# Four PSUM banks in one ring for projections and attention values, in place of three and one

## The chip, the cores and the metric

The kernel runs on one core of a Trainium2 chip. The metric is the device time of one execution in microseconds (us). Five engines work side by side, each through its own queue in order: TensorE (PE in the profile, with its weight loads as PEld), VectorE (DVE), ScalarE (ACT), GpSimd (POOL), and SyncE (SP), which here only starts transfers. Matmul results land in PSUM, which this kernel divides into eight banks of 128 partitions x 512 float32 numbers.

## The reference

One layer of a backbone for 1024 latent tokens and 256 context tokens of width 1024. Every token is normalised and modulated, then one input projection feeds three groups of heads, whose results are gated, put side by side and projected back:

```python
zl = jnp.split(hl @ w_in[l], PROJ_SPLITS, axis=-1)
zc = jnp.split(hc @ w_in[l], PROJ_SPLITS, axis=-1)
kc, vc = heads(zc[5]), heads(zc[6])
ya = short_conv_branch(zl[0], zl[1], zl[2], zl[3], conv_sc[l])
yb = neighbourhood_attention(heads(zl[4]), heads(zl[5]), heads(zl[6]), kc, vc, rpb[l])
yb = yb * jax.nn.silu(zl[7])
yc = conformer_branch(zl[8], zl[9], zl[10], conv_cf[l], conv_cf_b[l], ln_cf_g[l], ln_cf_b[l])
y = jnp.concatenate([ya, yb, yc], axis=-1) @ w_out[l]
x = x + gate[:, None, :] * y
```

`neighbourhood_attention` has 8 heads of 64 columns; each query looks at an 8 x 16 window of the 16 x 64 grid and at all context keys in one softmax.

## The kernel before, in words

Every matmul of a projection or of attention is split into high and low parts to keep float32 precision: a projection tile is 8 steps of three matmuls (lines 329 to 331), summed in one PSUM bank over 24 matmuls.

**Attention** goes by pairs of heads (four pairs), and in a pair by 16 blocks of 128 queries, 8 for each head. For block i `scores` (lines 596, 597) writes the scores to `ps_s`, DVE adds the bias and takes the minimum (601), ACT takes the exponential (604), DVE a reciprocal (605), POOL scales (606). Two blocks later `transposed` (615) turns the weights on PE into `ps_t`, and ACT and DVE (619, 620) copy them out as high and low parts `pw`. One step after that `values` (627) multiplies them with the values into a tile `po`. Two blocks, an even and an odd one, share a `po` tile; after the odd one `fold` reads it in three instructions: ACT 572, then DVE 576 and 578. The next even block opens the next `po`.

`attend` weaves these steps into projections. After each attention step three units of a projection (nine matmuls of 512 columns) follow on PE, so that a projection tile is spread over some three blocks. What remains of a pair's attention after its 16 steps runs as a coroutine during the projections of the next pair. Two more coroutines run beside attention: `conv_part`, the 31 taps of a convolution on DVE (line 692), and, in the last pair, `cf_norm`, which opens eight PSUM tiles of its own for transposes on PE (713 and 734) and waits in between for statistics and scaling on DVE and POOL.

**Order of work.** PE issues in the order in which the program is written. Outside `start` the order on DVE, ACT, POOL and SP is made by a planner at build time, which also hands out buffers: a tile of a pool gets the buffer that, by its plan, was freed first, and the first instruction that writes the new tile waits for the last readers of the old one.

**PSUM before.** `ps_s` and `ps_t` take two banks each. The pool `ps_z` has three banks; all projections, the value projection and `cf_norm` draw from it. The pool `ps_o` has one bank, for `po` alone. In `start`, `zb` holds the three `ps_z` banks and the `ps_o` bank for the first projections and for the matmuls of line 1000, which only keep PE busy. After attention the output projection has four banks `ps_f` in place of `ps_s` and `ps_t`.

Of the kernel before, what the change touches and what calls it, by code (L numbers as in the profile page):

```python
# [8 lines left out]
F32 = mybir.dt.float32  # L9
# [4 lines left out]
PSUM = bass.MemoryType.PSUM  # L14
DRAM = bass.MemoryType.DRAM

P = 128
# [5 lines left out]
HALF = 512  # L23
# [42 lines left out]
class Builder:  # L66
# [464 lines left out]
    def attention(self, pair):  # L531
        blocks = [(h, b) for h in range(2) for b in range(NB)]
        n = len(blocks)
        st = [None] * n
        vt, sg, kt = self.vt, self.sg, self.kt
        y = self.t2.tile([P, T], F32, name="yb", bufs=1)
        for i in range(n + LAG + 1):
            if i < n:
                h, b = blocks[i]
                if i == 0:  # L540
                    qv = [self.q_first]
                if b % 4 == QAH and i + 4 < n:
                    hn, bn = blocks[i + 4 - QAH]
                    qv.append(self.q_parts(hn, bn // 4))
                if b in (2, 4, 5) and 2 * pair + h < 7:
                    self.bias_tables(2 * pair + h + 1, (b - 1) // 2)
                st[i] = self.scores(kt, h, b, qv[i // 4])
            j = i - LAG
            if 0 <= j < n:
                st[j] = self.transposed(*st[j])  # L550
            j -= 1
            if j >= 0:
                h, b = blocks[j]
                if b % 2 == 0:
                    po = self.ps_o.tile([P, 2, 2, P], F32, name="po", tag="po")
                self.values(vt, h, b, st[j], po[:, b % 2])
                if b % 2 == 1:
                    self.fold(h, b // 2, po, y)
                if h == 1 and b % 4 == 3:
                    yg, sgg = (v.rearrange("p (r c) -> p r c", c=GW)[:, :, 8 * b - 24:8 * b + 8] for v in (y, sg))  # L560
                    self.nc.vector.tensor_tensor(out=yg, in0=yg, in1=sgg, op=ALU.mult)
                    if b == NB - 1:
                        self.nc.sync.dma_start(out=self.yd[2 + pair], in_=y)
            yield 2.5
# [487 lines left out]
    def build(self):  # L1052
# [13 lines left out]

        att = ExitStack()
        e, r = inp.enter_context, att.enter_context
        self.ps_z = e(self.pool("ps_z", 3, PSUM, side="right"))
        self.ps_o = e(self.pool("ps_o", 1, PSUM, side="right"))  # L1070
        self.u_cf, self.acc_cf, self.m_sc = {}, {}, {}
        hc = r(self.pool("hctx", 1, side="right"))
        self.h_ctx = [hc.tile([P, KT, TC], F32R, name=f"hc{i}") for i in range(2)]
# [7 lines left out]
        self.sp_b = q(self.pool("sp_b", 1, side="left"))  # L1081
        self.sp_w = stw.enter_context(self.pool("sp_w", 2, side="right"))
        zb = [self.ps_z.tile([P, HALF], F32, name="ps_z", tag="z") for _ in range(3)]
        zb.append(self.ps_o.tile([P, 2, 2, P], F32, name="po", tag="po").rearrange("p a b c -> p (a b c)"))

        def attn_pool():
            stw.close()
# [47 lines left out]
        with ExitStack() as st:  # L1135
            e = st.enter_context
# [78 lines left out]
```

## Time and profile before

| | |
|---|---|
| median of 3 runs | 612.09 us (611.95 to 612.26) |
| profiled execution | 610.97 us, of which 609.2 us are the span of the profile |
| PE busy, idle | 589.7 us, 19.5 us |
| DVE, ACT, POOL busy | 400.7, 245.9, 182.1 us |
| granted TensorE clock | 0.997 |
| attention of the four pairs, on PE | 166 to 222, 252 to 308, 338 to 393, 424 to 479 us |
| last projections, output projection | to 513 us, to the end |

The profile's busy time of PE counts a matmul until its modelled end. Matmuls overlap: one of 512 columns counts 0.39 us, but the next one starts 0.23 us after it. Idle time of PE in the profile is therefore what is left beyond the tail of the instruction before.

### The profile page before, as it was taken

How to read it: one execution, taken by the hardware profiler on the slowest of the kernel's cores; microseconds unless marked ns; L12 is line 12 of the kernel's file. 1: busy time of each engine (PE TensorE's matmuls, PEld its weight loads, DVE VectorE, ACT ScalarE, POOL GpSimd, SP SyncE). 2: the span in 40 equal slices, each digit the busy share in tenths (PEclk: the TensorE clock that was granted, in tenths of full speed). 3: DMA queues.
4: the chain of work that ended last, by engine and by line, in shares of the span. 5: the costliest groups of instructions: out<-in, count | busy, mean ns of one | idle time of the engine just before them, and what ended most of it. 6: DMA issues, size and time to landing. Idle time of an engine off the chain costs nothing.

```text
span 609.2 us, 8937 instructions
## 1 busy us (share of the span) xinstructions
PE 589.7 (97%) x3101; PEld 493.8 (81%) x3101; DVE 400.7 (66%) x681; ACT 245.9 (40%) x470; POOL 182.1 (30%) x194
## 2 busy tenths in 40 slices
PE   7899999999999999999999999999999999999995
PEld 5566888888888888888888888888788888888885
DVE  4466988765676699578897666936889447383222
ACT  2555822111455432544423554425645334124222
POOL 1021233000443222333112332113433370099311
PEclk9999999999999999999999999999999999999998
DMA  8992585976533136332145242172301454951122
GB/s 285 356 335 63 190 272 169 115 156 180 121 86 77 24 91 167 75 81 54 41 138 128 48 113 56 45 215 65 81 19 36 137 166 147 341 177 36 70 103 104
DMA packets 97170, 78.64 MB, mean 129 GB/s; under 512 B 26507, under 2 KB 80869, under 8 KB 96997
## 3 DMA queue, kind: packets, MB, share of 16 engines
q1 hardware_dynamic: 95397, 71.51, 42.4%
q10 hardware_dynamic: 1728, 6.55, 3.0%
q8 instruction: 25, 0.41, 0.3%
q14 instruction: 20, 0.16, 0.1%
HBM read 55.93 MB, written 14.29 MB: 115 GB/s over the span
## 4 chain that ended last, share of the span: by engine, by line
PE 84%; DVE 5%; ACT 3%; issue 2%; DMA 2%; POOL 2%; SPq 1%; POOLq 0%; DVEq 0%; ACTq 0%
PE ps_z L329 14%; PE ps_z L331 14%; PE ps_z L330 14%; PE po L627 5%; PE ps_f L878 5%; PE ps_f L879 5%; PE ps_f L877 5%; PE ps_t L615 4%; PE ps_z L419 3%; PE ps_z L421 3%; PE ps_s L596 3%; PE ps_z L420 3%; PE ps_s L597 2%; DMA wr<-in_w_in 2%; PE ps_h L279 1%
## 5 line engine op out<-in xcount | busy, mean ns | idle before, releaser
L329 PE MATMUL ps_z<-h,wh 128*128 128x512 f32 x384 | 151.1, 394 | 0.0
L331 PE MATMUL ps_z<-h,wl 128*128 128x512 f32 x384 | 150.3, 391 | 0.0
L330 PE MATMUL ps_z<-h,wh 128*128 128x512 f32 x384 | 149.8, 390 | 0.0
L130 POOL TENSOR_TENSOR wl<-wr,wh 128x512 fp32r<-128x512 f32 x44 | 60.8, 1384 | 167.3 <-ACT wh L129 160.3
L606 POOL TENSOR_SCALAR pr<-pr,sm 128x640 f32<-128x640 f32 (+1 forms) x64 | 56.6, 884 | 138.2 <-DVE sm L605 118.1
L331 PEld LDWEIGHTS ps_z<-h,wl 128*128 128x128 f32 x384 | 72.1, 188 | 16.1
L330 PEld LDWEIGHTS ps_z<-h,wh 128*128 128x128 f32 x384 | 72.1, 188 | 12.4
L329 PEld LDWEIGHTS ps_z<-h,wh 128*128 128x128 f32 x384 | 72.1, 188 | 12.1
L692 DVE SCALAR_TENSOR_TENSOR acc<-t,half_w,acc 128x1024 f32<-128x1024 f32 x60 | 81.1, 1351 | 1.2
L619 ACT ACTIVATE pw<-ps_t 128x640 fp32r<-128x640 f32 (+1 forms) x64 | 43.5, 680 | 90.1 <-PE ps_t L615 89.9
L601 DVE CUSTOM_DVE_ANT_0 ps_s<-ps_s,bt 128x640 f32<-128x640 f32 (+1 forms) x64 | 50.9, 796 | 29.4 <-PE ps_s L597 27.1
L620 DVE TENSOR_TENSOR pw<-ps_t,pw 128x640 fp32r<-128x640 f32 (+1 forms) x64 | 50.4, 788 | 16.0 <-ACT pw L619 15.8
L604 ACT ACTIVATE pr<-ps_s,mn 128x640 f32<-128x640 f32 (+1 forms) x64 | 49.0, 766 | 19.4 <-DVE mn L601 18.5
L627 PE MATMUL po<-pw,vt 128*128 128x256 f32 x304 | 51.3, 297 | 4.1 <-DVE yb L578 3.1
L878 PE MATMUL ps_f<-wol,y 128*128 128x512 f32 (+1 forms) x136 | 51.6, 379 | 0.0
L879 PE MATMUL ps_f<-woh,y 128*128 128x512 f32 (+1 forms) x136 | 51.5, 379 | 0.0
L877 PE MATMUL ps_f<-woh,y 128*128 128x512 f32 (+1 forms) x136 | 51.5, 379 | 0.0
L129 ACT ACTIVATE wh<-wr 128x512 fp32r<-128x512 f32 x46 | 29.0, 630 | 42.3 <-PE ps_z L330 21.0
L627 PEld LDWEIGHTS po<-pw,vt 128*128 128x128 f32 x304 | 40.5, 189 | 6.4 <-issue 4.7
L615 PE MATMUL ps_t<-ident,pr 128*128 128x128 f32 x304 | 43.6, 272 | 0.0
L596 PE MATMUL ps_s<-kt,qd 128*128 128x384 f32 (+1 forms) x128 | 39.6, 331 | 0.5 <-ACT pr L604 0.4
L615 PEld LDWEIGHTS ps_t<-ident,pr 128*128 128x128 f32 x304 | 35.6, 141 | 1.4 <-issue 0.4
(177 smaller groups left out, 923.9 us busy)
## 6 DMA issues: line engine op xcount, KB each, us to landing
wr<-in_w_in SPq DMA_DIRECT2D x52, 256.0 KB
wa<-in_w_ada SPq DMA_DIRECT2D x16, 512.0 KB
qd<-qn SPq DMA_DIRECT2D x32, 256.0 KB
vd<-t SPq DMA_DIRECT2D x20, 256.0 KB
x_in<-in_x SPq DMA_DIRECT2D x8, 512.0 KB
t<-in_w_ada SPq DMA_DIRECT2D x16, 256.0 KB
vt<-vd SPq DMA_DIRECT2D x32, 128.0 KB
fraw<-in_w_out SPq DMA_DIRECT2D x8, 512.0 KB
```

What stands on the lines that cost most here:

```text
L130: i2 = (eng or nc.vector).tensor_tensor(out=lo, in0=src, in1=f32(hi), op=ALU.subtract)
L329: nc.tensor.matmul(ps, lhsT=wh, rhs=hh, start=(k == 0), stop=False)
L330: nc.tensor.matmul(ps, lhsT=wh, rhs=hl, start=False, stop=False)
L331: self.last = nc.tensor.matmul(ps, lhsT=wl, rhs=hh, start=False, stop=(k == KT - 1))
L596: nc.tensor.matmul(win, lhsT=q[:, b % 4], rhs=kwin, start=(i == 0), stop=(i == 1))
L606: nc.gpsimd.tensor_scalar(out=pr, in0=pr, scalar1=sm, scalar2=0.5, op0=ALU.mult, op1=ALU.mult)
L615: nc.tensor.transpose(out=pt[:, c * P:(c + 1) * P], in_=pr[:, c * P:(c + 1) * P], identity=self.ident)
L627: self.nc.tensor.matmul(po, lhsT=vt[:, vi, h], rhs=pw[:, c], start=(c == 0), stop=(c == n - 1))
L692: self.after_pe(nc.vector.scalar_tensor_tensor(out=acc, in0=u[:, t:t + T], scalar=self.half_w[:, 2 * t + ct:2 * t + ct + 1], in1=acc, op0= ...
L877: nc.tensor.matmul(ps, lhsT=yh, rhs=wh[:, ch], start=(first and i == 0), stop=False)
L878: nc.tensor.matmul(ps, lhsT=yh, rhs=wl[:, ch], start=False, stop=False)
L879: nc.tensor.matmul(ps, lhsT=yl, rhs=wh[:, ch], start=False, stop=(last and i == len(chs) - 1))
```

## The change

`po` is no longer a pool of its own. `ps_z` has four banks, `po` is drawn from it under the same tag as the projections' tiles and seen as [2, 2, 128] for each partition, and the fourth tile of `zb` comes from it too. The number of banks, every instruction and its operands' shapes stay as they were.

```diff
                 if b % 2 == 0:
-                    po = self.ps_o.tile([P, 2, 2, P], F32, name="po", tag="po")
+                    po = self.ps_z.tile([P, HALF], F32, name="po", tag="z").rearrange("p (a b c) -> p a b c", a=2, b=2)
...
-        self.ps_z = e(self.pool("ps_z", 3, PSUM, side="right"))
-        self.ps_o = e(self.pool("ps_o", 1, PSUM, side="right"))
+        self.ps_z = e(self.pool("ps_z", 4, PSUM, side="right"))
...
         zb = [self.ps_z.tile([P, HALF], F32, name="ps_z", tag="z") for _ in range(3)]
-        zb.append(self.ps_o.tile([P, 2, 2, P], F32, name="po", tag="po").rearrange("p a b c -> p (a b c)"))
+        zb.append(self.ps_z.tile([P, HALF], F32, name="ps_z", tag="z"))
```

## The prediction

> **What bounds the kernel now.** I read the page first, then the waits of PE, then PE's order of time around the waits found.
>
> ```profile
> span 609.2 us, 8937 instructions
> PE 589.7 (97%) x3101; PEld 493.8 (81%) x3101; DVE 400.7 (66%) x681; ACT 245.9 (40%) x470; POOL 182.1 (30%) x194
> ...
> PEclk9999999999999999999999999999999999999998
> ```
>
> PE sets the time: busy for 97% of the span, at the full clock nearly everywhere. Whatever makes PE start its attention work sooner shortens the span, if nothing later gives it back. So the question is where PE waits for a `po` bank. The view of waits by engine, for PE (total us, times, longest):
>
> ```profile
> PE po L627 <- DVE yb L578: 3.1, 4, 1.0
> ...
> PE ps_z L734 <- DVE t L724: 0.9, 2, 0.5
> PE po L627 <- ACT pw L619: 0.8, 1, 0.8
> ...
> PE ps_s L596 <- ACT pr L604: 0.4, 2, 0.2
> ```
>
> Four times the first values matmul waits for line 578, the last reader of the `po` before. These are idle times after the modelled end of the transposes, so they are short of the true delay. I measure that by starts (a count of less than five after x is cut by the window asked for). PE's order of time, first an undelayed block with five transposes and one with four, then the delayed ones:
>
> ```profile
> 177.46 0.71 PE L615 MATMUL ps_t<-ident,pr 128*128 128x128 f32 x5
> 177.92 0.84 PE L627 MATMUL po<-pw,vt 128*128 128x256 f32 x5
> ...
> 447.58 0.60 PE L615 MATMUL ps_t<-ident,pr 128*128 128x128 f32 x4
> 447.93 0.61 PE L627 MATMUL po<-pw,vt 128*128 128x256 f32 x3
> ```
>
> ```profile
> 173.31 0.71 PE L615 MATMUL ps_t<-ident,pr 128*128 128x128 f32 x5
> 174.81 0.83 PE L627 MATMUL po<-pw,vt 128*128 128x256 f32 x5 [0.80 <-ACT pw L619]
> ...
> 302.94 0.60 PE L615 MATMUL ps_t<-ident,pr 128*128 128x128 f32 x4
> 304.56 0.83 PE L627 MATMUL po<-pw,vt 128*128 128x256 f32 x5 [1.03 <-DVE yb L578]
> ...
> 438.80 0.71 PE L615 MATMUL ps_t<-ident,pr 128*128 128x128 f32 x5
> 440.36 0.83 PE L627 MATMUL po<-pw,vt 128*128 128x256 f32 x5 [0.86 <-DVE yb L578]
> ...
> 462.44 0.71 PE L615 MATMUL ps_t<-ident,pr 128*128 128x128 f32 x5
> 463.90 0.48 PE L627 MATMUL po<-pw,vt 128*128 128x256 f32 x2 [0.76 <-DVE yb L578]
> ...
> 470.22 0.71 PE L615 MATMUL ps_t<-ident,pr 128*128 128x128 f32 x5
> 471.06 0.59 PE L627 MATMUL po<-pw,vt 128*128 128x256 f32 x3
> ```
>
> Undelayed, values start 0.46 us after the first of five transposes, 0.35 us after the first of four. At 174.81 the distance is 1.50, so 1.04 us are lost; at 304.56 it is 1.62, 1.27 lost; at 440.36, 463.90 and 471.06 1.10, 1.00 and 0.38. Ten even blocks in all show this, the first and the last of them above; the other five lose 0.25, 0.20, 0.25, 0.66 and 0.37. **The sum is 6.5 us: 3.67 in pairs 0 to 2 and 2.85 in pair 3.** The row at 174.81 names ACT, but DVE tells otherwise:
>
> ```profile
> 171.05 0.82 DVE L620 TENSOR_TENSOR pw<-ps_t,pw 128x640 fp32r<-128x640 f32 x1 [0.45 <-ACT pw L619]
> ...
> 174.25 0.41 DVE L578 TENSOR_TENSOR yb<-po,yb 64x256 f32<-64x256 f32 x1
> ...
> 302.67 1.29 DVE L692 SCALAR_TENSOR_TENSOR acc<-t,half_w,acc 128x1024 f32<-128x1024 f32 x1
> 303.99 0.43 DVE L578 TENSOR_TENSOR yb<-po,yb 64x256 f32<-64x256 f32 x1
> ```
>
> The weights `pw` of that block were ready at 171.87, 2.94 us early; line 578 ended at 174.66, 0.15 us before PE went on. The third row shows why a fold is late: it stands in DVE's queue behind a tap of the convolution that nobody waits for.
>
> **The change, part by part.** It adds and removes no instruction and no transfer; no DMA is moved past another by the edit itself. It removes one wait: an even block's values no longer wait for the fold of the pair of blocks just before. It adds two of the same kind: `po` may wait for a projection's sink, and a projection may wait for a fold.
>
> *The wait removed.* Ten delays, 6.5 us. What is late next when a delay goes? PE then reaches the next scores earlier by as much, and these wait for `ps_s`, which ACT must have read (line 604). The largest delay of pairs 0 to 2 that has scores behind it, and the tightest place of all:
>
> ```profile
> 174.71 0.79 ACT L604 ACTIVATE pr<-ps_s,mn 128x640 f32<-128x640 f32 x1
> ...
> 176.87 0.33 PE L596 MATMUL ps_s<-kt,qd 128*128 128x384 f32 x1
> ```
>
> ```profile
> 464.82 0.80 ACT L604 ACTIVATE pr<-ps_s,mn 128x640 f32<-128x640 f32 x1 [0.87 <-DVE mn L601]
> ...
> 466.62 0.33 PE L596 MATMUL ps_s<-kt,qd 128*128 128x384 f32 x1
> ```
>
> After the first delay `ps_s` is free at 175.50 and scores start at 176.87: 1.37 us of room, less about 0.15 for the signal, against 1.04 saved. The delay at 304.56 has no scores behind it, as its pair has none left. So I take pairs 0 to 2 in full: **3.67 us**. At the tightest place the room is 1.00 us for a saving of 1.00, so some 0.15 stays. Pair 3 is harder. Busy time by stretch, the four pairs' attention (PE, PEld, DVE, ACT, POOL, clock, DMA share, GB/s):
>
> ```profile
> 166.30:222.00 55.70, 54.69 (x329) 48.34 (x327) 41.18 (x81) 28.03 (x57) 18.86 (x20) 1.00 0.26 59
> 252.00:308.00 56.00, 54.77 (x327) 48.07 (x326) 43.56 (x86) 26.95 (x55) 15.92 (x17) 1.00 0.25 59
> 338.50:393.30 54.80, 54.39 (x327) 48.24 (x326) 39.51 (x81) 29.06 (x59) 17.44 (x19) 1.00 0.28 70
> 423.60:479.30 55.70, 52.70 (x327) 45.38 (x326) 46.30 (x106) 29.85 (x58) 20.42 (x25) 1.00 0.19 43
> ```
>
> DVE is busy for 41.18, 43.56 and 39.51 us of some 55 in pairs 0 to 2, but for 46.30 in pair 3, where `cf_norm` adds to it. There PE would lean on a DVE that is itself late, and a saved delay may come back as a wait for `pw`, `ps_t` or `cf_norm`'s scaling (the wait of L734 above). Bounds for pair 3: 0 and 2.85. I take the middle, **1.4 us**, since DVE's 9.4 free us there are between plenty and none.
>
> *The waits added.* For every tile I counted which earlier tiles of both kinds were still unread when PE opened it: never more than three. In pairs 0 to 2 the shortest time for which a bank of four would have stood free lies before 220.86; the tightest place of attention is in pair 3:
>
> ```profile
> 213.95 0.59 ACT L764 ACTIVATE t<-ps_z 128x512 f32<-128x512 f32 x1
> ...
> 220.86 0.39 PE L329 MATMUL ps_z<-h,wh 128*128 128x512 f32 x1
> ```
>
> ```profile
> 444.44 1.00 DVE L724 TENSOR_SCALAR t<-ps_z,bnmv,bnrs 128x256 f32<-128x256 f32 x2 [0.15 <-POOL bnrs L271]
> ...
> 446.48 0.67 DVE L767 TENSOR_TENSOR t<-ps_z,t 128x512 f32<-128x512 f32 x1
> 447.07 0.41 DVE L578 TENSOR_TENSOR yb<-po,yb 64x256 f32<-64x256 f32 x1
> ```
>
> ```profile
> 446.20 0.48 PE L329 MATMUL ps_z<-h,wh 128*128 128x512 f32 x1
> ```
>
> At 220.86 two banks are live, and the longer free of the others has been so since ACT left it at 214.54, over 6 us before. The projection tile opened at 446.20 finds three banks live and the fourth free since 445.44, 0.76 us before; the `po` at 447.93 could take the bank of line 767, free since 447.15, or that of line 578, free since 447.48. Behind a waiting PE instruction all of PE is queued. Cost: 0 at the old pace, up to some 1.5 us if PE arrives earlier by what the delays at 432 and 440 give back while DVE does not move. This is part of why pair 3 counts half; as a bound it goes into the range.
>
> *The planner's order.* DVE, ACT, POOL and SP are planned anew, and the plan sees other waits. An order that puts a fold, a minimum or a copy behind another 1.29 us tap (row of 302.67) costs PE up to that much at one place, or gains as much. Value taken: 0; bounds: 2 us either way, about one and a half taps.
>
> *After attention.* The chain that ended last runs through PE from there to the output. The loads of `w_out` and of the stored results follow the end of attention, so they move with it. Value: 0 lost; bounds 0 and 1 us.
>
> **Sum:** 3.67 + 1.4 = 5.1 us off a span of 609.2, that is 604.1, or 605.9 for the profiled execution, whose whole time is 610.97 (1.8 beside the span). The median of the runs is 612.09, 1.12 above that execution, so I predict 612.09 - 5.1 = **607.0 us**.
>
> **The rivals.**
>
> *All of it comes back:* 612.09 - 6.5 = 605.6 us. For it: `pw` is ready early and `ps_s` has room at nearly every place. Against: pair 3's DVE. Chance 0.17.
>
> *The gain turns into other waits:* DVE is the slower partner, its order stays unlucky, and only part of pairs 0 to 2 arrives, 1.3 to 3.5 us: 608.6 to 610.8 us. For it: the undelayed even blocks of pair 0 find the fold only 0.5 to 0.7 us early, so DVE is never far ahead. Against: the folds were early there all the same. Chance 0.13.
>
> *The change does nothing:* if the planner, by its own times, hands `po` the bank of the fold before in nearly every round, the waits stay: 612.1 us. For it: a bank is chosen by planned, not by true times. Against: two or three banks are free at most openings, that of the last fold being the one freed last. Chance 0.08.
>
> *Slower: the ring closes in pair 3.* One ring ties PE to the latest reader of either kind. There `cf_norm` opens eight tiles, and four `po` fall between them. If the planner gives these twelve tiles banks whose true release is late, PE waits for DVE each time; two such releases lie 0.33 us apart in the rows above (447.15, 447.48), a pass of line 724 takes 1.00. From 3.67 / 12 = 0.31 us each, with nothing saved in pair 3, the gain of the other pairs is gone; at 0.6 us each the time is 612.09 - 3.67 + 7.2 = 615.6 us. For it: three of four banks are live there. Against: the three banks before saw the same crowding, with 0.9 us of waits at L734 in all. Chance 0.07.
>
> *The clock falls.* All four attention stretches above have a clock of 1.00, with `ps_z` going round three banks. The Trainium skill ("TensorE: Matmul & The Clock Gate", section "A second HAM failure mode: psum-queue depth-cycling") reports a kernel where cycling through PSUM banks left PE idle so often for short times that its clock went down and up. By that rule the longer ring would be the risk. Here the matmuls of line 1000 show what a low clock costs:
>
> ```profile
> L1000 PE MATMUL po<-zero,ones_r x46: 392/396/795, 3.6 to 33.1; 128*128 128x512 f32 x46
> ```
>
> At most 795 ns against a median of 396, twice. If a tenth of the four stretches (22 us) ran so, some 11 us would be added: 618 us. Against: 6.5 us of pauses, none over 1.3, did not lower the clock. Chance 0.02.
>
> **How the numbers follow.** Forecast 0.53, all of it 0.17, other waits 0.13, nothing 0.08, ring 0.07, clock 0.02. Within 0.2% (1.2 us), about what a measurement of this kernel can tell from no change, lie "nothing" and a sliver of 0.01 of the others: faster 0.82 (0.53 + 0.17 + 0.13, less the sliver), same 0.09, slower 0.09 (ring and clock). The range goes from 605.0 (all of it, and a little luck in the order) to 610.8 us (the worst of other waits); the forecast's own is 605.8 to 608.5.
>
> **What would show it.** Right: no wait of L627 for L578; distances of 0.46 and 0.35 us in all even blocks of pairs 0 to 2; their stretches shorter by about 1.0, 1.7 and 0.9 us; DVE's share in pair 3 higher, with some new waits on L620, L604 or L724 there. Wrong: new waits of projections for L578, a later L601 or L620 in pairs 0 to 2, or a clock below 1.00 in attention.

## The result and the profile after

The changed kernel takes 607.32 us (median of 4 runs, 607.07 to 607.50) against 612.06 us: a ratio of 0.9922, 95% interval 0.9905 to 0.9939. The forecast was 607.0 us, in a range of 605.0 to 610.8. The ratios below leave out three executions that took 841 to 1515 us, two of e1 and one of e6. The profiled execution of the changed kernel took 607.07 us, of which 605.3 are the span. From the page and from the view of waits by engine for PE (total us, times, longest):

```profile
span 605.3 us, 8913 instructions
PE 587.7 (97%) x3101; PEld 493.2 (81%) x3101; DVE 400.1 (66%) x681; ACT 245.9 (41%) x470; POOL 182.8 (30%) x194
...
L627 PE MATMUL po<-pw,vt 128*128 128x256 f32 x304 | 51.4, 298 | 0.0
```

```profile
PE ps_z L734 <- DVE t L724: 1.0, 2, 0.7
PE ps_s L596 <- ACT pr L604: 0.9, 3, 0.5
PE ps_t L615 <- DVE sm L605: 0.6, 1, 0.6
```

The same group of instructions on the page of before, with its idle time and what ended it:

```profile
L627 PE MATMUL po<-pw,vt 128*128 128x256 f32 x304 | 51.3, 297 | 4.1 <-DVE yb L578 3.1
```

The line that carried the argument, L627 waiting for L578, is gone, and the idle time before L627 is 0.0 where it was 4.1. In its place stand longer waits on scores (0.9 where it was 0.4) and one on transposes (0.6, new). The two largest delays that pairs 0 to 2 had before, as they now stand in the trace of after: PE's order of time, and DVE beside it:

```profile
174.02 0.71 PE L615 MATMUL ps_t<-ident,pr 128*128 128x128 f32 x5
174.49 0.61 PE L627 MATMUL po<-pw,vt 128*128 128x256 f32 x3
...
302.16 0.60 PE L615 MATMUL ps_t<-ident,pr 128*128 128x128 f32 x4
302.51 0.72 PE L627 MATMUL po<-pw,vt 128*128 128x256 f32 x4
```

```profile
174.97 0.41 DVE L578 TENSOR_TENSOR yb<-po,yb 64x256 f32<-64x256 f32 x1
...
301.94 1.29 DVE L692 SCALAR_TENSOR_TENSOR acc<-t,half_w,acc 128x1024 f32<-128x1024 f32 x1
303.26 0.43 DVE L578 TENSOR_TENSOR yb<-po,yb 64x256 f32<-64x256 f32 x1
```

Values now start 0.47 and 0.35 us after the first transpose, the distances of an undelayed block, although the fold ends later than that (175.38 and 303.69). So do the values of all other even blocks, in pair 3 too: none of the ten delays is left. The tap still stands in front of the fold; PE no longer cares.

Where the time came from is seen best by stretches of PE's order, each from the start of one instruction to that of another. Here they are for the two kernels and, ahead of their discussion, for the experiments. A pair is the stretch from its first score to its last values matmul; "between" is the median of the three stretches from one pair to the next; "tail" goes from the last values to the first output matmul (line 877), "output" from there to the last matmul.

(The stretches of attention in the table of the kernel before begin later, some 9 us after the first scores of each pair.)

| us | to pair 0 | pair 0 | pair 1 | pair 2 | pair 3 | between | tail | output |
|---|---|---|---|---|---|---|---|---|
| before | 156.82 | 65.07 | 65.75 | 64.41 | 65.10 | 20.70 | 34.17 | 89.23 |
| after | 157.54 | 63.99 | 64.07 | 63.61 | 64.03 | 20.70 | 34.17 | 89.23 |
| one wait put back (e1) | 157.36 | 64.98 | 65.64 | 64.31 | 64.97 | 20.70 | 34.17 | 89.23 |
| two banks and two (e2) | 160.81 | 63.96 | 64.08 | 63.65 | 70.54 | 21.77 | 37.64 | 89.23 |
| ring of three (e3) | 158.26 | 63.99 | 64.10 | 63.63 | 64.90 | 20.70 | 34.17 | 89.27 |
| folds first (e4) | 158.05 | 65.05 | 64.37 | 64.30 | 64.73 | 20.70 | 34.17 | 89.23 |
| gate product on POOL (e6) | 157.04 | 63.99 | 64.07 | 63.61 | 63.29 | 20.70 | 34.17 | 89.23 |
| both edits, pair 3 (e9) | 157.53 | 64.00 | 64.07 | 63.62 | 62.21 | 20.70 | 34.17 | 89.23 |

The change took 1.08, 1.68, 0.80 and 1.07 us out of the four pairs, **4.63 us together, and nothing anywhere else**. The spans differ by only 3.9 because this execution needed 0.72 us more ahead of attention. That part differs from run to run (156.82 to 158.26 in the rows above other than e2), with PE waiting there for loads of `w_ada` and `c_ctx`, 3.9 us in before and 5.0 in after; the difference of the medians, 4.74 us, is close to the 4.63 of the pairs.

The planned orders differ hardly at all: on POOL and SP not one instruction stands elsewhere; on DVE one line 578 and on ACT one line 572, both near the end of pair 3, have changed places with a neighbour. Pairs 0 to 2 gave what was predicted. Pair 3 gave 1.07 of 2.85 us, and why is half of the question below.

### The profile page after: what moved, and what is told of

Same layout as the page of the kernel before. It is cut to its first block, busy times and chain, and to the rows that moved or that the text cites. A ratio compares the mean times of both kernels' runs of the same rounds, so it can differ in the third digit from the quotient of the medians.

```text
span 605.3 us, 8913 instructions
## 1 busy us (share of the span) xinstructions
PE 587.7 (97%) x3101; PEld 493.2 (81%) x3101; DVE 400.1 (66%) x681; ACT 245.9 (41%) x470; POOL 182.8 (30%) x194
## 4 chain that ended last, share of the span: by engine, by line
PE 86%; DVE 4%; ACT 3%; POOL 2%; issue 1%; DMA 1%; SPq 1%; POOLq 0%; DVEq 0%; ACTq 0%
PE ps_z L329 14%; PE ps_z L331 14%; PE ps_z L330 14%; PE po L627 5%; PE ps_t L615 5%; PE ps_f L878 5%; PE ps_f L879 5%; PE ps_f L877 5%; PE ps_s L596 3%; PE ps_z L419 3%; PE ps_z L421 3%; PE ps_z L420 3%; PE ps_s L597 2%; DMA wr<-in_w_in 1%; PE ps_h L279 1%
## 5 line engine op out<-in xcount | busy, mean ns | idle before, releaser
L627 PE MATMUL po<-pw,vt 128*128 128x256 f32 x304 | 51.4, 298 | 0.0
L627 PEld LDWEIGHTS po<-pw,vt 128*128 128x128 f32 x304 | 40.5, 190 | 0.3
```

The costliest lines, as they stand in the source:

```text
L627: self.nc.tensor.matmul(po, lhsT=vt[:, vi, h], rhs=pw[:, c], start=(c == 0), stop=(c == n - 1))
```

## The experiments

Theory for the gain: the wait for the fold before was all of it. Rivals: the planner's new order, or the number of banks, did part. Theory C for what pair 3 kept back: `cf_norm` crowds DVE, as the prediction had it. Theory S, from reading the trace of after: it is other work near the end of the pair.

**e1: the wait put back, the ring kept.** The first values matmul of an even block gets a dependency on line 578 of the fold before:

```diff
-                self.values(vt, h, b, st[j], po[:, b % 2])
+                first = self.values(vt, h, b, st[j], po[:, b % 2])
+                if b % 2 == 0 and self.folded is not None:
+                    self.tc.add_manual_dep(first.ins, self.folded.ins.name,
+                                           mybir.DependencyInfo(mybir.DependencyClass.Sync, mybir.DependencyReason.DATA),
+                                           reason="fold")
                 if b % 2 == 1:
-                    self.fold(h, b // 2, po, y)
+                    self.folded = self.fold(h, b // 2, po, y)
...
```

> The changed kernel with one wait put back: an even block's first values matmul waits again for line 578 of the fold before, while po stays in the ring of four. Theory (the wait alone is the change; the planned order of DVE and ACT differs from before in two places only): the ten delays return, 611.5 to 612.5 us. Rival (banks or order did part of it): a time between, 608.5 to 611 us.

Measured: 611.52 us, ratio to before 0.9996 (0.9987 to 1.0005). PE's waits in this kernel, whose lines are five to eight further down:

```profile
PE po L632 <- DVE yb L583: 3.5, 5, 1.0
...
PE ps_z L742 <- DVE t L732: 0.9, 2, 0.5
PE ps_s L601 <- ACT pr L609: 0.4, 2, 0.2
```

All four pairs are back near the lengths of before, 0.09 to 0.13 us short of them, and PE waits for the fold at the same ten blocks. So 4.20 of the 4.63 us hang on this one wait. That 0.43 do not come back fits a quicker release: in nine of the ten blocks values start 0.06 us after the fold ends, where in before it was 0.15 in all ten. Why it is quicker stays open.

**e2: two banks for projections, two for `po`.**

```diff
-        self.ps_z = e(self.pool("ps_z", 3, PSUM, side="right"))
-        self.ps_o = e(self.pool("ps_o", 1, PSUM, side="right"))
+        self.ps_z = e(self.pool("ps_z", 2, PSUM, side="right"))
+        self.ps_o = e(self.pool("ps_o", 2, PSUM, side="right"))
...
```

> Two banks for the projections and two for po, apart. Theory: po with two banks loses its ten delays (6.5 us, 4.6 of them kept), but by the tiles of before two banks are too few for the projections: in the trace of before 14 of their tiles open before the second bank would be free, 22 us together, above all in the value projection (2.0 and 0.2), pair 3 (7.5) and the last projections (7.8). 612.06 - 4.6 + 10 to 20 = 617 to 627 us. Rival (a second po bank is all that counts, the projections don't care): 607 to 608 us.

Measured: 624.95 us, ratio 1.0214 (1.0198 to 1.0231).

```profile
PE ps_z L329 <- DVE kt L380: 5.1, 4, 2.7
PE ps_z L329 <- DVE sm L605: 2.8, 1, 2.8
PE ps_z L329 <- DVE t L391: 2.4, 1, 2.4
```

Two banks serve `po` fully: pairs 0 to 2 are as short as with the ring. But projections now wait for their own sinks, in every other stretch: 5.4 us longer in pair 3 than before, 3.5 in the tail, some 3 to 4 ahead of pair 0, 1.1 between pairs. A fixed split of the four banks is worse than the ring either way.

Not all of pair 3 is waiting, though. Behind the longest wait of this kernel's attention the granted clock fell, which it did in none of the other traces kept here while PE had work in attention. PE's order of time, and the view of busy time by stretch (PE, PEld, DVE, ACT, POOL, clock, DMA share, GB/s):

```profile
426.99 0.47 PE L329 MATMUL ps_z<-h,wh 128*128 128x512 f32 x1 [2.78 <-DVE sm L605]
...
428.95 0.63 PE L330 MATMUL ps_z<-h,wh 128*128 128x512 f32 x1
429.37 0.63 PE L331 MATMUL ps_z<-h,wl 128*128 128x512 f32 x1
```

```profile
425.00:428.00 3.00, 1.01 (x5) 0.87 (x6) 2.22 (x5) 1.17 (x3) 1.53 (x3) 1.00 0.00 0
428.40:431.70 3.30, 3.30 (x12) 2.92 (x12) 0.59 (x1) 0.00 (x0) 0.00 (x0) 0.50 0.00 0
```

(The first row names line 605, but PE waited for a bank of `cf_norm`: line 724, which reads it, ended 0.15 us before.) For 3.4 us the clock was 0.50, and matmuls of 512 columns started 0.43 us apart in place of 0.23, which by an estimate from these rows is 1.6 us of the 5.4. The other three executions of e2 took 1.4 to 2.9 us longer than this one, at a mean granted clock of 0.987 to 0.990 against 0.996; they were not traced. The waits of 2.7 us at 81.90 and 2.4 at 514.49 were followed by no such fall, so the length of a wait alone does not tell.

**e3: a ring of three, the fourth bank used in `start` alone.**

```diff
-        self.ps_z = e(self.pool("ps_z", 4, PSUM, side="right"))
+        self.ps_z = e(self.pool("ps_z", 3, PSUM, side="right"))
+        self.ps_o = e(self.pool("ps_o", 1, PSUM, side="right"))
...
-        zb.append(self.ps_z.tile([P, HALF], F32, name="ps_z", tag="z"))
+        zb.append(self.ps_o.tile([P, HALF], F32, name="spare", tag="spare"))
```

> One ring of three banks for projections and po; the fourth bank serves start alone. Theory (never more than two live in pairs 0 to 2, three in pair 3): pairs 0 to 2 keep their gain of 3.6 us; in pair 3 seven tiles of the changed kernel's trace open before the third bank would be free, 5 us together, partly overlapping: 608.5 to 612 us, all of the loss between 420 and 450 us. Rival (the fourth bank is needed everywhere): over 614 us. Rival (three do as well): 607.3 us.

Measured: 608.15 us, ratio 0.9941 (0.9929 to 0.9954), a little under the expected 608.5. Pairs 0 to 2 are as with four banks; pair 3 is 0.87 us longer. PE's order of time there:

```profile
428.37 0.63 PE L734 MATMUL ps_z<-ident,t 128*128 128x128 f32 x4 [1.08 <-DVE t L724]
...
444.83 0.50 PE L329 MATMUL ps_z<-h,wh 128*128 128x512 f32 x1 [0.89 <-DVE t L767]
```

The second row is a projection that waits for a bank which line 767 still reads, as counted. Of the 5 us counted from starts and releases most did not stay. Against the trace of after, PE's starts in pair 3 fall back by 3.0 us in all, mostly at these two rows (1.24 and 1.14), but 2.1 of them are won back at once, because PE then comes late enough not to wait at the next L734. So it is the sharing, not a fourth bank, that pays in pairs 0 to 2; the fourth is worth 0.9 us, in the pair with `cf_norm`.

**e4: the kernel before, folds ahead in the plan.**

```diff
                 if b % 2 == 1:
-                    self.fold(h, b // 2, po, y)
+                    with self.tc.high_priority(400):
+                        self.fold(h, b // 2, po, y)
```

> The kernel before (three banks and one), but the planner is told to serve the fold's three instructions ahead of everything else that is ready. Theory (folds were late because they stood in DVE's queue behind taps and sinks): most of the ten delays shrink, though what now stands behind the folds may be late in its turn: 608.5 to 610.5 us. Rival (the fold is late by its own chain of ACT and two DVE instructions, whatever the order): 611.5 to 612.5 us.

Measured: 610.27 us, ratio 0.9970 (0.9960 to 0.9980). DVE at the place of the largest delay, lines one further down than before:

```profile
302.50 0.43 DVE L577 TENSOR_TENSOR yb<-po,fold 64x256 f32<-64x256 f32 x1
302.96 0.82 DVE L621 TENSOR_TENSOR pw<-ps_t,pw 128x640 fp32r<-128x640 f32 x1
303.82 0.43 DVE L579 TENSOR_TENSOR yb<-po,yb 64x256 f32<-64x256 f32 x1
304.28 2.60 DVE L693 SCALAR_TENSOR_TENSOR acc<-t,half_w,acc 128x1024 f32<-128x1024 f32 x2
```

Both taps now come after the fold, and pair 1 is 1.38 us shorter. Pair 0 is not shorter at all, pairs 2 and 3 by 0.11 and 0.37. So order explains part of the lateness, and this order repairs 1.9 of the 4.6 us. It does not show that the rest needs the bank: at the delay of pair 0 a tap and a minimum (lines 693 and 602) still stand ahead of the fold's two instructions, as they did before, so the request moved only some of the folds. Whether an order that moves all of them would do as much was not tested.

**What pair 3 kept back.** In the trace of after two waits stand near the end of pair 3, when `cf_norm` is over. First DVE, then PE:

```profile
462.50 1.17 DVE L783 SCALAR_TENSOR_TENSOR t<-t,convc,t 128x512 f32<-128x512 f32 x1
463.59 0.82 DVE L601 CUSTOM_DVE_ANT_0 ps_s<-ps_s,bt 128x640 f32<-128x640 f32 x1
...
467.67 0.69 DVE L561 TENSOR_TENSOR yb<-yb,sg 128x512 f32<-128x512 f32 x1
468.39 0.82 DVE L620 TENSOR_TENSOR pw<-ps_t,pw 128x640 fp32r<-128x640 f32 x1
```

```profile
465.50 0.39 PE L596 MATMUL ps_s<-kt,qd 128*128 128x256 f32 x1 [0.49 <-ACT pr L604]
...
468.36 0.39 PE L331 MATMUL ps_z<-h,wl 128*128 128x512 f32 x1
469.36 0.74 PE L615 MATMUL ps_t<-ident,pr 128*128 128x128 f32 x5 [0.61 <-DVE sm L605]
```

By starts these two cost 0.65 and 0.77 us. A tap of the short convolution (line 783) stands ahead of the minimum (601) that frees `ps_s` for the scores; the gate product (561) stands ahead of the copy (620) that frees `ps_t`: 620 ends at 469.21, and the transposes start 0.15 us later. The row names `sm`, but it is the copy that came last.

**e5: without `cf_norm`** (a single execution; the kernel leaves out the transposes, statistics and scaling):

```diff
             if pair == 3:
-                self.spawn(self.cf_norm(), 6.0)
+                pass
```

> The changed kernel without cf_norm, so the conformer branch enters the output unnormalised and unswished; its transposes, statistics and scaling in pair 3 are left out. Theory C (cf_norm's load on DVE is why pair 3 kept only 1.1 of its 2.85 us): the waits of the changed kernel in pair 3, 0.65 us on scores (L596) and 0.77 us on transposes (L615) near its end, go too. Theory S (they come from the short convolution's taps, lines 781 and 783, and the gate product, line 561, which stand in DVE's queue at the end of pair 3, after cf_norm is over): both waits stay, 1.0 to 1.5 us together. The time itself falls by PE's 64 transposes (some 7 us) either way.

Measured: 601.48 us. PE's waits within pair 3:

```profile
PE ps_s L596 <- ACT pr L604: 0.8, 2, 0.6
PE ps_t L615 <- DVE sm L605: 0.2, 1, 0.2
```

With `cf_norm` gone, 1.1 us of idle time of the same two kinds remains in pair 3, against 1.2 with it (0.12 at the pair's third scores, 0.49 and 0.61 in the rows above). But it does not stand at the same places:

```profile
416.88 0.44 PE L596 MATMUL ps_s<-kt,qd 128*128 128x384 f32 x1 [0.59 <-ACT pr L604]
...
456.86 0.44 PE L596 MATMUL ps_s<-kt,qd 128*128 128x384 f32 x1 [0.26 <-ACT pr L604]
...
463.49 0.74 PE L615 MATMUL ps_t<-ident,pr 128*128 128x128 f32 x5 [0.22 <-DVE sm L605]
```

The first of these rows is the 0.12 of after, grown because four transposes of `cf_norm` that PE did just before these scores are gone. Near the end 0.26 and 0.22 us are left of 0.49 and 0.61: the wait for scores is shorter and comes one block earlier, that for transposes has lost 0.39 us by starts. Theory S had both staying, with 1.0 to 1.5 us, so it holds only in part. The waits near the end do not need `cf_norm`, but without it they are about half as long, and the planner's order moved too. How much of them is due to `cf_norm` this run leaves open. (The expectation counted 64 transposes; `cf_norm` has 32, and pair 3 was 6.2 us shorter in all.)

**e6: the gate product on POOL. e7: the taps held back. e8: both.**

```diff
-                    self.nc.vector.tensor_tensor(out=yg, in0=yg, in1=sgg, op=ALU.mult)
+                    self.nc.gpsimd.tensor_tensor(out=yg, in0=yg, in1=sgg, op=ALU.mult)
```

```diff
-            nc.vector.tensor_scalar(out=a, in0=m[:, t0:t0 + HALF], scalar1=w[0], scalar2=None, op0=ALU.mult)
+            self.after_pe(nc.vector.tensor_scalar(out=a, in0=m[:, t0:t0 + HALF], scalar1=w[0], scalar2=None,
+                                                  op0=ALU.mult))
             for t in (1, 2):
-                nc.vector.scalar_tensor_tensor(out=a, in0=m[:, t0 + t:t0 + t + HALF], scalar=w[t], in1=a,
-                                               op0=ALU.mult, op1=ALU.add)
+                self.after_pe(nc.vector.scalar_tensor_tensor(out=a, in0=m[:, t0 + t:t0 + t + HALF], scalar=w[t],
+                                                             in1=a, op0=ALU.mult, op1=ALU.add))
```

> The changed kernel with the gate product (line 561, eight instructions of 0.69 us) on POOL in place of DVE. Theory S: the wait of 0.77 us for transposes at the end of pair 3 goes, as DVE's copy of the block before moves up by the 0.69 us of line 561; pairs 0 to 2 stay as they are: 606.4 to 606.9 us. Theory C: no difference, 607.1 to 607.6 us.

> The changed kernel with the three taps of the short convolution (lines 781 and 783) held back on DVE until the last matmul of their projection has been issued; the projection's bank is kept some 2 us longer. Theory S: the waits of 0.65 and 0.13 us for scores near the end of pair 3 go, unless the taps meet another block's work at their new place: 606.3 to 607.2 us. Theory C: no gain, 607.1 to 608 us.

> Both edits at once, the gate product on POOL and the taps held back. Theory S: both waits go, 605.7 to 606.6 us, the fastest of all. Theory C: no gain, 607.1 to 608 us.

Measured, ratios to before: e6 606.47 us, 0.9916 (0.9902 to 0.9930); e7 606.66 us, 0.9921 (0.9908 to 0.9934); e8 606.46 us, 0.9914 (0.9900 to 0.9928). These times lie too close to that of the change to part the theories; the stretches do. In e6, POOL, DVE and PE at the place of the second wait:

```profile
467.20 1.29 POOL L561 TENSOR_TENSOR yb<-yb,sg 128x512 f32<-128x512 f32 x1 [0.87 <-DVE yb L578]
```

```profile
467.15 0.82 DVE L620 TENSOR_TENSOR pw<-ps_t,pw 128x640 fp32r<-128x640 f32 x1
```

```profile
467.86 0.40 PE L331 MATMUL ps_z<-h,wl 128*128 128x512 f32 x1
468.12 0.74 PE L615 MATMUL ps_t<-ident,pr 128*128 128x128 f32 x5
```

The copy follows line 578 at once, the transposes come 0.26 us after the matmul before them in place of 1.00, and pair 3 takes 63.29 us in place of 64.03: 0.74 us off, every other pair unchanged. In e7 pair 3 falls by 1.43 us, to 62.60, since the held taps no longer stand ahead of lines 601 and 620. But pair 2 rises by 1.32, to 64.93: the copy of the keys comes late after the taps held back in pair 1, and the first scores of pair 2 wait for it:

```profile
PE ps_s L597 <- DVE kt L380: 0.9, 1, 0.9
```

In e8 pair 3 takes 62.25 us and pair 2 64.51. With `cf_norm` in place, removing the gate product and the taps from DVE's queue there is enough to remove both waits: to that extent theory S holds.

**e9: the gate product on POOL, the taps held back in pair 3 alone.** As e8, but with the dependency only for the second half of the channels, whose taps fall into pair 3:

```diff
...
+            for ins in taps if ct else ():
+                self.after_pe(ins)
...
```

> The gate product on POOL, and the taps held back in pair 3 alone (second half of the short convolution's channels). By theory S the 0.71 to 1.06 us that holding the taps in pair 1 cost at the start of pair 2 are not paid here, and pair 3 takes 62.3 us in place of 64.0: 605.4 to 605.9 us, the fastest version. Rival (the small gains of such edits do not add up): 606.2 to 607.3 us.

Measured: 605.23 us (605.20 to 605.35), ratio 0.9898 (0.9884 to 0.9911), the fastest. Pairs 0 to 2 stay at the change's lengths, and pair 3 falls by 1.82 us to 62.21. What PE still waits for from attention on:

```profile
PE ps_z L734 <- DVE t L724: 1.0, 2, 0.7
...
PE ps_s L596 <- ACT pr L604: 0.4, 2, 0.2
```

The intervals of this ratio and of the change's own (0.9905 to 0.9939) just overlap; the length of pair 3 decides.

**e10: the same two edits on the kernel before.**

> The same two edits on the kernel before, with three banks and one. Theory (there the waits stand at the fold, and in pairs 0 to 2 neither edit moves it forward; only in pair 3, where a tap stood between the fold's instructions, some comes back): 0.5 to 1.5 us off, 610.3 to 611.3 us, so most of the change's gain is still to be had beside it. Rival (a lighter DVE does what the banks do): under 609 us.

Measured: 611.11 us, ratio 0.9991 (0.9982 to 1.0000).

```profile
PE po L627 <- DVE yb L578: 1.7, 3, 0.9
...
PE po L627 <- ACT pw L619: 1.4, 2, 0.8
```

This lighter DVE does not do what the shared banks do: PE goes on waiting before L627, and the edits that take 1.82 us out of pair 3 of the changed kernel take 0.43 out of that of the kernel before. Its whole time falls by 0.6 (611.67 for the kernel before in the same runs, less 611.11), in an interval that reaches up to no change.

## Why the prediction was right

*The bound and the wait.* PE's ten delays, 6.5 us by starts, were the right quantity: all ten are gone, and e1 brings them back by putting back one wait. The idle column alone would have given 4.1 us at most, less than the 4.63 that came, since it begins only at the modelled end of the transposes.

*Pairs 0 to 2 in full.* Predicted 3.67 us, measured 3.56 (1.08 + 1.68 + 0.80). The room on scores was enough, as read.

*Pair 3 at less than half.* Predicted 1.4 of 2.85 us, measured 1.07. The 1.4 was the middle between nothing and all, not the outcome of a sum, so that it came near is luck, and with it that the whole is only 0.3 us off. Compared start by start, all four delays of pair 3 went (2.82 us), and 1.78 us came back on PE: 0.24 and 0.75 at two scores, 0.66 at the transposes, 0.13 at L734. Such places had been named in advance, and DVE's share of pair 3 did rise, from 80.3% of the stretch to 81.8%, though hardly more than in the other pairs (0.7 to 1.1 points there). What was wrong is the reading of the room on scores. The prediction called 466.62 the tightest place and expected 0.15 us to stay there; 0.24 did. The very next scores of before had less room, 0.27 us:

```profile
468.68 0.80 ACT L604 ACTIVATE pr<-ps_s,mn 128x640 f32<-128x640 f32 x1
```

```profile
469.74 0.28 PE L596 MATMUL ps_s<-kt,qd 128*128 128x256 f32 x1
```

These are the scores that lost 0.75. Wrong in part was also the reason, the load of `cf_norm` and of DVE in general: the two large waits come after `cf_norm` has ended, each behind a single place in DVE's queue, a tap and a gate product that nobody yet waited for. e9 takes them out and with them 1.65 of the 1.78 us; the 0.13 at L734 stays, and the rest of its 1.82 had been lost in the kernel before as well. That `cf_norm` plays no part is not shown (e5). The view of busy time by stretch (46.30 of 55.7 us) pointed to the right engine and the right pair, not to the instructions.

*The waits added.* Put at 0, with up to 1.5 in pair 3: four banks added none that can be seen. Three banks added 0.87 us, at the kind of place that was named.

*The planner's order.* Put at 0, bounds 2: it came out nearly unchanged.

*After attention.* Put at 0: tail and output are equal to 0.01 us.

*The rivals.* None came. "All of it" failed by pair 3. "Other waits" laid them into pairs 0 to 2, which kept 3.56 us; they came in pair 3 alone. "The change does nothing" is what e1 looks like: the wait for the fold stays. The ring did not close with four banks; with three (e3) it costs 0.87 us, in pair 3 as that rival had it. The clock did not fall in the changed kernel. The clock in the attention stretches of after, pairs 2 and 3 by the view of busy time by stretch (the clock stands after POOL):

```profile
327.00:390.70 63.70, 63.70 (x379) 56.44 (x378) 44.69 (x93) 33.34 (x68) 20.32 (x23) 1.00 0.28 70
411.30:475.30 64.00, 61.54 (x377) 53.09 (x376) 52.40 (x123) 33.32 (x66) 22.87 (x30) 1.00 0.20 47
```

It stays at 1.00, so the Trainium skill's second failure mode of the clock gate ("TensorE: Matmul & The Clock Gate", section "A second HAM failure mode: psum-queue depth-cycling") did not show here with a ring of four. The prediction priced a low clock at twice the time by the longest matmul of line 1000, which is the first of them; at the clock of 0.50 in e2 matmuls of 512 columns started 0.43 us apart in place of 0.23, 1.9 times. Whether that fall, behind one long wait, is the same failure mode is not shown.

## What to carry to other kernels

Where two kinds of tile of one size take turns, and one has banks that stand free while the other waits, let them share a ring before asking for more banks: here three shared banks did in three pairs of four what four banks split three and one did not do, and split two and two did only with a larger loss elsewhere. Count delays on a pipelined engine by distances of starts against an undelayed repetition, not by the idle column, and look at what the next wait's releaser was queued behind: here the next wait, when one had gone, came from a single instruction that nobody needed yet, standing ahead of one that somebody did.

## What was not expected of the hardware

The stretches repeat far better than the whole: pair 0 took 63.99, 63.96, 63.99, 63.99 and 64.00 us in the executions of after, e2, e3, e6 and e9, while the part ahead of attention, where PE waits for its first loads, took 157.04 to 158.26 in the same ones other than e2. A comparison by stretch of single profiled executions told differences of 0.1 us apart that the medians of several runs could not.
